# A hybrid encoder layer: seven-product parts for blocks 0 to 11 of the first down-projection, and all weight sums on GpSimd

## The chip, the cores and the metric

The kernel runs on one core of a Trainium2 chip. TensorE multiplies matrices and accumulates them in the banks of PSUM; VectorE, ScalarE and GpSimd work on tiles in SBUF; SyncE (SP) issues most of the DMA transfers, ScalarE some. The metric is the device time of one execution in microseconds (us), as the median of several runs.

## What is computed

One layer of a streaming encoder, in float32, over 2112 tokens (a prompt of 2048 and a sample of 64), with 1024 features and a hidden width of 2816:

```python
mod = (c_act @ w_ada + b_ada)[:, None, :]
sh1, sc1, gt1, sh2, sc2, gt2 = jnp.split(mod, 6, -1)
h = rmsnorm(x, g1) * (1 + sc1) + sh1
proj = h @ w_in                                  # pooling inputs u, and q, k, v, o, gates
pool_out, pool_buf_new = pool_mixer(u, pool_buf, start, w_pool, s_pool)
hs, C, n, m = mlstm_seq(q, k * HEAD_DIM ** -0.5, v, ig, lf, C, n, m)
...
mix = jnp.concatenate([pool_out, hs], -1) @ w_out
x = x + gt1 * mix                                # end of the attention half
h2 = rmsnorm(x, g2) * (1 + sc2) + sh2
up = h2 @ w_up                                   # (T, 2 * 2816)
conv = b_conv + sum(w_conv[j] * upp[:, j:j + T] for j in range(3))
a, g = jnp.split(conv, 2, -1)
x = x + gt2 * ((jax.nn.silu(g) * a) @ w_down)    # the down-projection
```

The states of the pooling mixer, the mLSTM and the convolution are outputs too.

## The kernel before, in words

Features lie on the partitions and tokens along the rows. Every weight is split into two rounded parts, high and low, so that a float32 product is three passes of the fast format: ScalarE copies the high part (L428), VectorE subtracts to get the low part (L431).

**The attention half** takes the tokens in four groups, three of 512 and a last of 576. Within a group come the projections, the four mLSTM heads, the pooling mixer, and the output projection, which runs two rows of 128 features at a time (eight rows; 16 units of weights `wo_in` and `w_out`, loaded by SP into `raw`). For each row x is loaded (`scr<-xT`, L608), the product is added to it on VectorE, the row is stored (`x2d<-scr`, L661), and its squares are summed into `ssum` (L522 for row 0, L525 and L526 for the others). A pair of rows takes the four PSUM banks `mm`, two for each row, so row 5 uses the banks that row 3's addition sets free. In this half a scheduler orders the instructions of each engine from the program's order and its own estimates; what is marked `keep_in_program_order` keeps its place.

Side work is written as generators in five lists, `bg[0]` to `bg[4]`. A tick takes one step of a list's first generator, and `drain` runs lists until they are empty. `bg[4]` holds `up_sums` from the second group on. It makes the sums of weights that the Strassen products of the FFN's up-projection need: 22 blocks of two column halves are 44 pieces, each with two loads of `w_up` into a tile `w4` (four buffers), four sums of 128x256, and a store to `wsum` in HBM. Three pieces are loaded ahead.

**From attention to FFN.** After the matmuls of rows 0 and 1 of the last group's output projection, `between()` is called, which there is `leave()`: it drains the lists 1 to 4, gives the attention half's memory back (the pool `a1`, with `w4` in it, among it), opens the FFN's pool `f1` in that memory, and appends `norm_sums`. That one makes the sums of the first FFN group's operands: for each of four column pairs it loads `h2d` into `fscr` (issued by ScalarE, L829), and makes seven operands, each with two high copies on ScalarE (L809 into `hx`) and low parts and differences on VectorE (L795, L791).

**The FFN half** takes the tokens in three groups of 704, which are three squares of two halves of 352. In this half the order of all engines is written out by hand. The up-projection of each of the 22 blocks takes seven products instead of eight (L1616). The down-projection is done in parts of blocks, listed in `PARTS`. A part of four blocks is done in seven products too (`Quad`, `quad_down`, L2084): 168 matmuls of 352 columns, with weight sums `dsum`. A part of six is an ordinary product (L2230): 288 matmuls, alternately of 448 and 256 columns. The first group has the parts (0, 6), (6, 12), (12, 16), (16, 22); the other two have (0, 4), (4, 8), (8, 12), (12, 16), (16, 22). The weight sums `dsum` are made in the first group by `quad_sums`: 16 pieces, each with one load from `w_quad` into a tile `qs`, four sums of 128x256 on VectorE, and a store to `dsum` (the lists `SUMS` say which are made when).

Of the kernel before, what the change touches and what calls it, by code (L numbers as in the profile page):

```python
# [9 lines left out]
F32 = mybir.dt.float32  # L10
F32R = mybir.dt.float32r
# [5 lines left out]
P = 128  # L17
# [7 lines left out]
NF = 22  # L25
# [7 lines left out]
PARTS = (((0, 6), (6, 12), (12, 16), (16, 22)), ((0, 4), (4, 8), (8, 12), (12, 16), (16, 22)),  # L33
         ((0, 4), (4, 8), (8, 12), (12, 16), (16, 22)))
NQ, QUADS = 4, 4
SUMS = ((6, 7, 0, 1, 2), (3, 4, 5))
# [30 lines left out]
def tile_layer(ctx: ExitStack, tc: tile.TileContext, xT, vecs, cst, rst, w_mod, w_ada, w_qkou, w_v, w_pool,  # L67
# [799 lines left out]
    if True:  # L867
# [6 lines left out]
        def up_sums():  # L874

            def load(f, c):
                w = a1.tile([P, 4, 256], F32, tag="w4", name="w4", bufs=4)
                for i in range(2):
                    tc.keep_in_program_order(nc.sync.dma_start(out=w[:, 2 * i:2 * i + 2, :], in_=w_up[NF * i + f].rearrange(
                        "p (h c) -> p h c", h=2)[:, :, c:c + 256]))  # L880
                return w
            todo = [(f, c) for f in range(NF) for c in (0, 256)]
# [3 lines left out]
            def store():  # L886
                if made:
                    f, c, w = made.pop()
                    pin(nc.sync.dma_start(out=wsum[f, :, :, c:c + 256], in_=w))
            yield  # L890
            yield
            for i, (f, c) in enumerate(todo):
                w = nx.pop(0)
                yield
                yield

                a0, a1_, g0, g1 = (w[:, i, :] for i in range(4))
                pin(dve.tensor_tensor(out=g1, in0=g0, in1=g1, op=ALU.add))
                pin(dve.tensor_tensor(out=g0, in0=a0, in1=g0, op=ALU.subtract))
                yield  # L900
                store()
                pin(dve.tensor_tensor(out=a0, in0=g1, in1=a0, op=ALU.subtract))
                pin(dve.tensor_tensor(out=a1_, in0=a1_, in1=a0, op=ALU.subtract))
                made.append((f, c, w))
                yield
                if 0 < i and i + 2 < len(todo):
                    nx.append(load(*todo[i + 2]))
# [758 lines left out]
    def quad_sums(ds):  # L1666

        for d in ds:
            for c in (0, 256):
                t = f2.tile([P, 2, FT], F32R, tag="av", name="qs", bufs=AVB)  # L1670
                w = t.bitcast(F32).rearrange("p a t -> p (a t)")[:, :1024].rearrange("p (i c) -> p i c", i=4)
                nc.sync.dma_start(out=w, in_=w_quad[d, :, :, c:c + 256])
                for _ in range(7):
                    yield
                a11, a12, a21, a22 = (w[:, i] for i in range(4))
                dve.tensor_tensor(out=a22, in0=a21, in1=a22, op=ALU.add)
                yield
                dve.tensor_tensor(out=a21, in0=a11, in1=a21, op=ALU.subtract)
                yield
                dve.tensor_tensor(out=a11, in0=a22, in1=a11, op=ALU.subtract)  # L1680
                yield
                dve.tensor_tensor(out=a12, in0=a12, in1=a11, op=ALU.subtract)
                yield
                yield
                nc.sync.dma_start(out=dsum[d, :, :, c:c + 256], in_=w)
                yield
                yield

# [474 lines left out]
    for o in fgroups:  # L2163
        Bo = B[o.g]
        held = None
        for pi, part in enumerate(PARTS[o.g]):
# [6 lines left out]
            if quad is not None and o.g == 0:  # L2173
                drain(0)
                aside, bg[1][:] = list(bg[1]), []
            if pi == 0:
                pair = None
            for f in range(f0, f1_):
                old, pair = pair, Pair(o, Bo, f, f - f0, av, quad)
                pair.products(old)  # L2180
                if o.g == 0 and f == 2:
                    bg[0].append(quad_sums(SUMS[0]))
# [3 lines left out]
                if held is not None and nf > 2:  # L2186
                    quad_down(o, held, pair, old)
                    held = None
                    if o.g == 0:
                        bg[0].append(quad_sums(SUMS[1]))  # L2190
                        bg[1].extend(aside)
# [199 lines left out]
```

## Time and profile before

| | |
|---|---|
| time, median of 3 runs | 2168.68 us (2167.97 to 2169.99) |
| span of the profiled execution | 2165.8 us; the page gives no other time of its own for it, and the median of the runs is 2.9 us above |
| TensorE busy | 2143.9 us, 99% |
| VectorE, ScalarE busy | 1649.8 and 1105.2 us, 76% and 51% |
| GpSimd busy | 265.3 us, 12% |
| the attention half ends | with the output projection's last matmul, at 787.0 us |

A row of a profile gives a line of the kernel, an engine, an operation, the tiles out and in, and a count; then the busy time and the mean of one in ns, and the idle time ahead of them with what ended it. In a timeline the first number is the start in us and the second the length. "<-" in brackets names what an engine had waited for. The lines shown with an L are those of the kernel before.

### The profile page before, as it was taken

Reading aid. Unit: us, or ns where it says so; the run is one execution under the profiler, and the core shown is the slowest. Engines: PE = TensorE matmul, PEld = TensorE weight load, DVE = VectorE, ACT = ScalarE, POOL = GpSimd, SP = SyncE. Lnnn points to the kernel's source line nnn. Section 1 sums busy time; section 2 is a strip of 40 time slices with the busy share of each in tenths; the row PEclk is TensorE's granted clock in tenths of the full one; section 3 lists DMA queues with packets and bytes.
Section 4 is the critical chain, followed back from the end, with each engine's and each line's share of the span. In section 5 each row is a group of like instructions: output and inputs, shape, how many; then the busy total and the mean of one; then the engine's idle time right before and its main releaser. Section 6 shows DMA issues by size and latency. Waiting matters only on the chain.

```text
span 2165.8 us, 38050 instructions
## 1 busy us (share of the span) xinstructions
PE 2143.9 (99%) x13529; PEld 2038.3 (94%) x13529; DVE 1649.8 (76%) x3060; ACT 1105.2 (51%) x2193; POOL 265.3 (12%) x475
## 2 busy tenths in 40 slices
PE   8999999999999999999999999999999999999998
PEld 7888888888899999999999999999999999999998
DVE  5777679677675778788688768988877597887874
ACT  4554335234333557465556445655655365565554
POOL 0010000001000301010001220100101321111112
PEclk9999999999999999999999999999999999999999
DMA  8987997897799689797768976665668675555542
GB/s 320 331 304 225 325 311 249 292 325 259 247 294 296 207 273 317 241 343 248 229 219 305 360 282 207 228 225 202 219 234 276 221 251 190 171 175 188 172 159 76
DMA packets 297063, 541.09 MB, mean 250 GB/s; under 512 B 25728, under 2 KB 113280, under 8 KB 296872
## 3 DMA queue, kind: packets, MB, share of 16 engines
q1 hardware_dynamic: 286280, 513.44, 70.3%
q10 hardware_dynamic: 10592, 25.20, 3.0%
q8 instruction: 107, 1.75, 0.3%
q14 instruction: 84, 0.69, 0.1%
HBM read 412.56 MB, written 125.98 MB: 249 GB/s over the span
## 4 chain that ended last, share of the span: by engine, by line
PE 89%; DVE 4%; DMA 3%; issue 1%; ACT 1%; SPq 0%; POOL 0%; POOLq 0%; DVEq 0%; ACTq 0%
PE mm L1616 37%; PE mm L495 23%; PE mm L2230 11%; PE mm L2084 10%; PE mm L1155 3%; DVE wt L431 1%; PE m L1345 1%; PE m L1365 1%; PE m L1367 1%; PE m L1330 1%; DMA wt<-dsum 0%; PE mm L1091 0%; DMA qs<-w_quad 0%; DVE tg L1594 0%; DMA raw<-w_up 0%
## 5 line engine op out<-in xcount | busy, mean ns | idle before, releaser
L1616 PE MATMUL mm<-hx,wt 128*128 128x352 f32 x5544 | 886.1, 321 | 2.5 <-DVE wt L431 2.2
L1616 PEld LDWEIGHTS mm<-hx,wt 128*128 128x128 f32 x5544 | 878.3, 188 | 4.9 <-DVE wt L431 4.2
L495 PE MATMUL mm<-hl,wt 128*128 128x512 f32 (+2 forms) x1920 | 385.4, 356 | 0.0
L431 DVE TENSOR_TENSOR wt<-raw,wt 128x512 fp32r<-128x512 f32 (+1 forms) x460 | 310.8, 681 | 79.1 <-ACT wt L428 77.7
L428 ACT ACTIVATE wt<-raw 128x512 fp32r<-128x512 f32 (+1 forms) x460 | 274.7, 604 | 168.0 <-PE mm L495 53.2
L495 PEld LDWEIGHTS mm<-hl,wt 128*128 128x128 f32 x1920 | 314.7, 188 | 47.4 <-issue 4.4
L2084 PE MATMUL mm<-av,wt 128*128 128x352 f32 x1512 | 248.0, 323 | 1.7 <-DVE x L2053 0.7
L2084 PEld LDWEIGHTS mm<-av,wt 128*128 128x128 f32 x1512 | 242.3, 188 | 4.8 <-DVE ea L1625 2.8
L2230 PE MATMUL mm<-av,wt 128*128 128x448 f32 (+1 forms) x1440 | 231.4, 322 | 0.0
L2053 DVE SCALAR_TENSOR_TENSOR x<-mm,MOD,x 128x352 f32<-128x352 f32 (+3 forms) x368 | 171.9, 507 | 77.8 <-PE mm L2230 62.0
L2230 PEld LDWEIGHTS mm<-av,wt 128*128 128x128 f32 x1440 | 220.8, 188 | 9.7
L1664 ACT ACTIVATE mm<-mm 128x352 f32<-128x352 f32 x204 | 91.4, 448 | 238.9 <-PE mm L1616 175.1
L495 PE MATMUL mm<-mx,wt 128*128 128x512 f32 (+1 forms) x960 | 182.6, 352 | 0.0
L495 PEld LDWEIGHTS mm<-mx,wt 128*128 128x128 f32 x960 | 159.3, 188 | 22.5
L1594 DVE SCALAR_TENSOR_TENSOR ta<-ea,V,ta 128x704 f32<-128x704 f32 (+1 forms) x132 | 125.7, 953 | 60.4 <-ACT ta L1589 56.3
L1594 DVE SCALAR_TENSOR_TENSOR tg<-eg,V,tg 128x704 f32<-128x704 f32 (+1 forms) x132 | 125.7, 952 | 49.8 <-ACT tg L1589 47.2
L431 DVE TENSOR_TENSOR wt<-wt 128x512 fp32r<-128x512 f32 x204 | 138.7, 685 | 10.9 <-ACT wt L428 10.7
L428 ACT ACTIVATE wt<-wt 128x512 fp32r<-128x512 f32 x204 | 123.8, 622 | 25.9 <-DMA wt<-wsum 24.7
L1572 POOL COPY ea<-UC 128x2 f32<-128x2 f32 x66 | 35.0, 530 | 529.1 <-DVE ta L1594 418.4
L1812 ACT ACTIVATE tg<-tg 128x704 f32<-128x704 f32 (+1 forms) x66 | 52.5, 796 | 71.3 <-DVE tg L1594 71.3
L1155 PE MATMUL mm<-wt,hl 128*128 128x256 f32 (+1 forms) x576 | 71.2, 284 | 0.0
L1155 PEld LDWEIGHTS mm<-wt,hl 128*128 128x128 f32 x576 | 70.3, 189 | 0.8 <-issue 0.6
(305 smaller groups left out, 2222.7 us busy)
## 6 DMA issues: line engine op xcount, KB each, us to landing
wt<-wsplit SPq DMA_DIRECT2D x132, 512.0 KB, 4.2
raw<-w_up SPq DMA_DIRECT2D x198, 256.0 KB, 4.1
wt<-hl_kept SPq DMA_DIRECT2D x96, 512.0 KB, 5.9
wt<-wsum SPq DMA_DIRECT2D x132, 256.0 KB, 4.9
wsplit<-wt SPq DMA_DIRECT2D x66, 512.0 KB, 5.3
w<-w_up SPq DMA_DIRECT2D x88, 256.0 KB, 4.7
wsum<-w SPq DMA_DIRECT2D x44, 512.0 KB, 5.3
Bd<-fscr ACTq DMA_DIRECT2D x56, 352.0 KB, 3.4
```

The costliest lines, as they stand in the source:

```text
L428: act.activation(u.w[:, 0, :u.n], u.raw[:, :u.n], AF.Copy)
L431: dve.tensor_tensor(out=u.w[:, 1, :u.n], in0=u.raw[:, :u.n], in1=u.w[:, 0, :u.n].bitcast(F32), op=ALU.subtract)
L495: pe.matmul(ps[bi][:, :hi - lo], U[:, a, k % 4 * P:(k % 4 + 1) * P], mv[k][:, b, lo:hi], start=(at == 0 and pi == 0), stop=(k == order[-1] ...
L1155: pe.matmul(ps[ti][:n, :cols], h[4 * kh + k4][:, b, lo:lo + n], U[:, a, k4 % 2 * cols:(k4 % 2 + 1) * cols], start=(kh == 0 and k4 == 0 and ...
L1572: pool.tensor_copy(ext[:, 0:2], UC[:, f, :])
L1594: dve.scalar_tensor_tensor(out=t[:, :E], in0=ext[:, j:j + E], scalar=wc(j, f), in1=t[:, :E], op0=ALU.mult, op1=ALU.add)
L1616: pe.matmul(bk.t[:, :FH], U[:, a, kc * P:(kc + 1) * P], Bo.at(nm, kc, b), start=(first and kc == 0 and pi == 0), stop=(kc == 3 and pi == 2 ...
L1664: act.activation(to.t[:, :FH], bk.t[:, :FH], AF.Copy)
L1812: act.activation(self.tg[:, :E], self.tg[:, :E], AF.Silu)
L2053: dve.scalar_tensor_tensor(out=x3[n][:, a:b], in0=bk.t[:, a - lo:b - lo], scalar=gt2(n, s), in1=x3[n][:, a:b], op0=ALU.mult, op1=ALU.add)
L2084: pe.matmul(bk.t[:, :FH], U[:, a, c:c + P], quad.put(op, m, b), start=(first and m == 0 and pi == 0), stop=(m == 1 and pi == 2), skip_grou ...
L2230: pe.matmul(bks[i].t[:, :hi - lo], U[:, a, k % 4 * P:(k % 4 + 1) * P], av[k][:, b, lo:hi], start=(k == 0 and (a, b) == PASSES[0]), stop=(k ...
```

## The change

The first FFN group gets the same parts as the other two, so blocks 0 to 11 become three seven-product parts in place of two ordinary ones. `quad_sums` and its lists go; the 16 pieces of `w_quad` are appended to `up_sums`, behind its 44, with the same tile, one load each and a store to `dsum`. All its sums, of both kinds, are given to GpSimd in place of VectorE. The operands of the second FFN group (`prepare`) are no longer put aside while the first group's `dsum` are finished.

```diff
--- before.py
+++ after.py
@@ -30,10 +30,9 @@
 EB = 1
 AVB = 7
 ENDS = ((0, 448), (448, 704))
-PARTS = (((0, 6), (6, 12), (12, 16), (16, 22)), ((0, 4), (4, 8), (8, 12), (12, 16), (16, 22)),
+PARTS = (((0, 4), (4, 8), (8, 12), (12, 16), (16, 22)), ((0, 4), (4, 8), (8, 12), (12, 16), (16, 22)),
          ((0, 4), (4, 8), (8, 12), (12, 16), (16, 22)))
 NQ, QUADS = 4, 4
-SUMS = ((6, 7, 0, 1, 2), (3, 4, 5))
 
 
 def paired(g, part):
@@ -875,18 +874,22 @@
 
             def load(f, c):
                 w = a1.tile([P, 4, 256], F32, tag="w4", name="w4", bufs=4)
+                if f >= NF:
+                    tc.keep_in_program_order(nc.sync.dma_start(out=w, in_=w_quad[f - NF, :, :, c:c + 256]))
+                    return w
                 for i in range(2):
                     tc.keep_in_program_order(nc.sync.dma_start(out=w[:, 2 * i:2 * i + 2, :], in_=w_up[NF * i + f].rearrange(
                         "p (h c) -> p h c", h=2)[:, :, c:c + 256]))
                 return w
-            todo = [(f, c) for f in range(NF) for c in (0, 256)]
+            todo = [(f, c) for f in range(NF + 2 * QUADS) for c in (0, 256)]
             pin = tc.keep_in_program_order
             nx, made = [load(*todo[i]) for i in range(3)], []
 
             def store():
                 if made:
                     f, c, w = made.pop()
-                    pin(nc.sync.dma_start(out=wsum[f, :, :, c:c + 256], in_=w))
+                    to = wsum[f] if f < NF else dsum[f - NF]
+                    pin(nc.sync.dma_start(out=to[:, :, c:c + 256], in_=w))
             yield
             yield
             for i, (f, c) in enumerate(todo):
@@ -895,12 +898,12 @@
                 yield
 
                 a0, a1_, g0, g1 = (w[:, i, :] for i in range(4))
-                pin(dve.tensor_tensor(out=g1, in0=g0, in1=g1, op=ALU.add))
-                pin(dve.tensor_tensor(out=g0, in0=a0, in1=g0, op=ALU.subtract))
+                pin(pool.tensor_tensor(out=g1, in0=g0, in1=g1, op=ALU.add))
+                pin(pool.tensor_tensor(out=g0, in0=a0, in1=g0, op=ALU.subtract))
                 yield
                 store()
-                pin(dve.tensor_tensor(out=a0, in0=g1, in1=a0, op=ALU.subtract))
-                pin(dve.tensor_tensor(out=a1_, in0=a1_, in1=a0, op=ALU.subtract))
+                pin(pool.tensor_tensor(out=a0, in0=g1, in1=a0, op=ALU.subtract))
+                pin(pool.tensor_tensor(out=a1_, in0=a1_, in1=a0, op=ALU.subtract))
                 made.append((f, c, w))
                 yield
                 if 0 < i and i + 2 < len(todo):
@@ -1662,29 +1665,6 @@
     def seed(to, bk):
 
         act.activation(to.t[:, :FH], bk.t[:, :FH], AF.Copy)
-
-    def quad_sums(ds):
-
-        for d in ds:
-            for c in (0, 256):
-                t = f2.tile([P, 2, FT], F32R, tag="av", name="qs", bufs=AVB)
-                w = t.bitcast(F32).rearrange("p a t -> p (a t)")[:, :1024].rearrange("p (i c) -> p i c", i=4)
-                nc.sync.dma_start(out=w, in_=w_quad[d, :, :, c:c + 256])
-                for _ in range(7):
-                    yield
-                a11, a12, a21, a22 = (w[:, i] for i in range(4))
-                dve.tensor_tensor(out=a22, in0=a21, in1=a22, op=ALU.add)
-                yield
-                dve.tensor_tensor(out=a21, in0=a11, in1=a21, op=ALU.subtract)
-                yield
-                dve.tensor_tensor(out=a11, in0=a22, in1=a11, op=ALU.subtract)
-                yield
-                dve.tensor_tensor(out=a12, in0=a12, in1=a11, op=ALU.subtract)
-                yield
-                yield
-                nc.sync.dma_start(out=dsum[d, :, :, c:c + 256], in_=w)
-                yield
-                yield
 
     def half_tile(nm):
         return f1.tile([P, FH], F32, tag=nm, name=nm)
@@ -2170,25 +2150,18 @@
             ends = o.last and lastp
             av = [None] * nf
             quad = Quad() if paired(o.g, part) else None
-            if quad is not None and o.g == 0:
-                drain(0)
-                aside, bg[1][:] = list(bg[1]), []
             if pi == 0:
                 pair = None
             for f in range(f0, f1_):
                 old, pair = pair, Pair(o, Bo, f, f - f0, av, quad)
                 pair.products(old)
                 if o.g == 0 and f == 2:
-                    bg[0].append(quad_sums(SUMS[0]))
                     bg[1].append(prepare(fgroups[1], fscr))
                 if o.g == 0 and len(x3) < KD or pi == 0 and not bg[0]:
                     x3 += load_x2(o, range(len(x3), min(len(x3) + 2, KD)))
                 if held is not None and nf > 2:
                     quad_down(o, held, pair, old)
                     held = None
-                    if o.g == 0:
-                        bg[0].append(quad_sums(SUMS[1]))
-                        bg[1].extend(aside)
             if pi == 0 and o.g > 0:
                 drain(0)
                 x3 += load_x2(o, range(len(x3), KD))
```

What the change does to the order of the instructions shows at the passage from attention to FFN. In the new kernel the lines of the same code have numbers a few lower; `w_7815`, `w_8001` and so on are tiles `w4`, each holding one piece.

GpSimd in the new kernel, where the pooling mixer of the last group ends:

```order
L1429 COPY PO<-u 128x15
L1430 COPY PO<-u 128x15
L901 TENSOR_TENSOR w_7815<-w_7815 128x256
L902 TENSOR_TENSOR w_7815<-w_7815 128x256
L905 TENSOR_TENSOR w_7815<-w_7815 128x256
L906 TENSOR_TENSOR w_7815<-w_7815 128x256
L901 TENSOR_TENSOR w_8001<-w_8001 128x256
L902 TENSOR_TENSOR w_8001<-w_8001 128x256
```

In this manner it goes on for 64 sums, down to the piece `w_8283`; in the kernel before, the FFN's first instruction (a memset of `UC`) stands in this place.

SP at the same passage, before, from the last store into `wsum` on:

```order
L889 DMA wsum<-w_7587 512x1x256
L771 DMA h2d<-mx_6358 128x352
L1458 DMA o_pool<-PO 128x120
L608 DMA scr<-xT 128x576
L407 DMA raw<-w_out 128x512
L407 DMA raw<-wo_in 128x512
L407 DMA raw<-w_out 128x512
L407 DMA raw<-wo_in 128x512
L661 DMA x2d<-scr 128x576
L407 DMA raw<-w_out 128x512
L661 DMA x2d<-scr 128x576
L608 DMA scr<-xT 128x576
```

SP in the new kernel, where the load of x for row 2 is followed by the first store into `dsum`:

```order
L1461 DMA o_pool<-PO 128x120
L607 DMA scr<-xT 128x576
L892 DMA dsum<-w_7815 512x1x256
L878 DMA w_8199<-w_quad 128x4x256
L892 DMA dsum<-w_8001 512x1x256
L878 DMA w_8206<-w_quad 128x4x256
```

and the end of the same run:

```order
L878 DMA w_8276<-w_quad 128x4x256
L892 DMA dsum<-w_8262 512x1x256
L878 DMA w_8283<-w_quad 128x4x256
L892 DMA dsum<-w_8269 512x1x256
L892 DMA dsum<-w_8276 512x1x256
L892 DMA dsum<-w_8283 512x1x256
L660 DMA x2d<-scr 128x576 x2
L607 DMA scr<-xT 128x576
L660 DMA x2d<-scr 128x576
L406 DMA raw<-wo_in 128x512
L406 DMA raw<-w_out 128x512
L406 DMA raw<-wo_in 128x512
```

Sixteen stores and thirteen loads now stand ahead of the stores of rows 0 and 1, the load of x for row 3, and the last five loads of the output projection's weights.

ScalarE, before, where the loads of `norm_sums` come (`mx` and `u` belong to the attention half, `wt` to the weights' split):

```order
L517 ACTIVATE mx_7615<-scr 128x576
L428 ACTIVATE wt<-raw 128x512
L517 ACTIVATE mx_7614<-scr 128x576
L829 DMA fscr<-h2d 128x704 x4
L428 ACTIVATE wt<-raw 128x512
L809 ACTIVATE hx<-fscr 128x352 x4
L428 ACTIVATE wt<-raw 128x512
L522 ACTIVATE ssum<-scr 128x576
```

and in the new kernel:

```order
L427 ACTIVATE wt<-raw 128x512
L516 ACTIVATE mx_7614<-scr 128x576
L427 ACTIVATE wt<-raw 128x512 x4
L524 ACTIVATE scr<-scr 128x576
L521 ACTIVATE ssum<-scr 128x576
L828 DMA fscr<-h2d 128x704 x4
L808 ACTIVATE hx<-fscr 128x352 x2
L427 ACTIVATE wt<-raw 128x512
```

The loads `fscr<-h2d` and all copies of `norm_sums` have moved behind the squares of rows 0 and 1 (L524, L521). The instruction at L521 waits there for the last transfer of every DMA queue ahead of it, the last store into `dsum` among them, and for GpSimd's last sum.

## The prediction

> **What bounds the kernel now.** I read the page's head with its list of engines, then the waits of TensorE, then the windows.
>
> ```profile
> span 2165.8 us, 38050 instructions
> PE 2143.9 (99%) x13529; PEld 2038.3 (94%) x13529; DVE 1649.8 (76%) x3060; ACT 1105.2 (51%) x2193; POOL 265.3 (12%) x475
> ```
> The waits of TensorE (sum, count and mean in us):
> ```profile
> PE m L1054 <- DMA mx<-xT: 5.5, 1, 5.5
> PE mm L1616 <- DVE wt L431: 2.2, 3, 1.1
> ```
> TensorE is idle for 2165.8 − 2143.9 = 22 us of the span, and its longest waits are of this size. So matmuls taken away shorten the time one for one, as long as everything that feeds them stays ahead; and a feed that comes late shows in full. The median of the runs, 2168.7, is 2.9 us over the span of the profiled execution; I work in the span and add the 2.9.
>
> **What is removed from TensorE.** The chain that ended last has, of the opening group, the first ordinary part of six blocks (L2230) and its part of four in seven products (L2084):
>
> ```profile
> 867.03 3.88 PE mm L2230 x24
> ...
> 872.81 41.99 PE mm L2230 x264
> ...
> 1105.31 4.03 PE mm L2084 x24
> ...
> 1111.24 23.05 PE mm L2084 x144
> ```
> Blocks 0 to 11 cost 2 × (3.88 + 41.99) = 91.7 us before, and 3 × (4.03 + 23.05) = 81.2 us after: **−10.5 us**. Nothing else covers TensorE there, so all of it counts.
>
> **The sums on GpSimd.** The 176 sums of w_up leave VectorE (four lines of this kind), the 64 of w_quad leave it in the opening FFN group, and all 240 go to GpSimd. VectorE's price is the first row, from the lines between 220 and 740 us; GpSimd's are its only two-input groups of this size:
>
> ```profile
> L902 DVE TENSOR_TENSOR w<-w 128x256 f32<-128x256 f32 x44 | 18.6, 422 | 0.8
> ```
> ```profile
> L2045 POOL TENSOR_TENSOR ssum<-ssum,fscr 128x256 f32<-128x256 f32 x4 | 2.9, 736 | 8.8 <-ACT fscr L2044 8.8
> ...
> L2033 POOL TENSOR_TENSOR y<-x,fscr 128x256 f32<-128x256 f32 x2 | 1.4, 726 | 2.0 <-ACT fscr L2001 2.0
> ```
> A piece is four sums: 4 × 0.422 = 1.7 us on VectorE, 4 × 0.726 = 2.9 us on GpSimd, which gets 240 × 0.726 = 174 us of work. The windows of core 0 (columns: window, length, then PE, PEld, DVE, ACT and POOL, then clock, DMA share, GB/s):
>
> ```profile
> 220.00:740.00 520.00, 519.24 (x3197) 460.10 (x3196) 379.20 (x822) 204.00 (x515) 45.48 (x56) 1.00 0.85 280
> 1041.00:1105.00 64.00, 64.00 (x406) 63.92 (x405) 48.61 (x74) 41.39 (x76) 8.22 (x16) 1.00 0.72 235
> ```
> For 220 to 740, where the 44 pieces of w_up lie, TensorE already runs 519.24 of 520 us, so the 176 × 0.42 = 74 us that VectorE sheds can win under 1 us. It can lose: two operations side by side are slow in this trace.
>
> ```profile
> 722.96 8.33 POOL L1426 COPY PO<-u 128x15 f32<-128x15 f32 x1 [1.20 <-ACT u L267]
> ...
> 738.93 0.80 POOL L1427 COPY PO<-u 128x15 f32<-128x15 f32 x1
> ```
> ```profile
> 1228.13 1.71 POOL L2045 TENSOR_TENSOR ssum<-ssum,fscr 128x704 f32<-128x704 f32 x1 [2.39 <-ACT fscr L2044]
> ```
> ```profile
> 1228.54 1.84 DVE L431 TENSOR_TENSOR wt<-raw,wt 128x512 fp32r<-128x512 f32 x1 [1.05 <-ACT wt L428]
> ```
> The same split takes 0.69 us as a rule (x14, from the lines between 740 and 800 us):
>
> ```profile
> L431 DVE TENSOR_TENSOR wt<-raw,wt 128x512 fp32r<-128x512 f32 x14 | 9.6, 686 | 6.3 <-ACT wt L428 6.3
> ```
> Beside GpSimd's add it took 1.84, 1.16 more. If one in ten of the 176 sums cost TensorE that much, it is 20 us. Bounds −1 to +20; VectorE has 27% of this stretch idle, so I take **+2**. The Trainium skill has the same rule (GPSIMD Engine Reference, section Key points): GpSimd shares its SBUF interfaces with VectorE and contends with VectorE instructions of two SBUF inputs. The trace agrees, and the rule speaks against this change; what it would make of it is rival C.
>
> In the opening FFN group VectorE loses 64 × 0.42 = 27 us of sums, and takes on the handling of three seven-product parts for two ordinary ones. The window from 1041 to 1105 shows such a group's work at 48.6 of 64 us with TensorE never idle. I take 0, with +5 as the upper end; work of the next group's operands now lies over these parts.
>
> **Sixteen pieces of w_quad do not fit into the attention half.** This is the large term. The order of the new kernel shows that 13 of the 16 come out as one run where the last attention group hands over to the FFN half: on GpSimd behind the last copy into PO, 64 sums in a row; on SP a store of dsum and a load of w_quad in turns, each store waiting for GpSimd, each load for an older store (four buffers). SP issues in order, and behind this run stand the row x2d and scr<-xT of row 3, and five of the output projection's 16 weight loads. On ScalarE, L521 (square sum) waits for all DMA under way and for GpSimd's last sum, because the FFN's pool takes the memory of the w4 tiles; behind it stand the loads fscr<-h2d and the copies of norm_sums, which makes the FFN's first operands. What stands there before:
>
> ```profile
> 739.76 0.34 SPq L1458 DMA_DIRECT2D o_pool<-PO  x1
> ...
> 753.52 0.42 SPq L608 DMA_DIRECT2D scr<-xT  x1
> ...
> 754.04 0.42 SPq L407 DMA_DIRECT2D raw<-wo_in  x1
> ```
> ```profile
> 735.76 51.36 PE L495 MATMUL mm<-mx,wt 128*128 128x256 f32 x384
> 786.96 2.08 PE L1616 MATMUL mm<-hx,wt 128*128 128x352 f32 x12
> 789.03 10.61 PE L1616 MATMUL mm<-hx,wt 128*128 128x352 f32 x66
> ```
> ```profile
> 742.19 2.22 ACTq L829 DMA_DIRECT2D fscr<-h2d  x4
> 747.39 0.50 ACT L809 ACTIVATE hx<-fscr 128x352 fp32r<-128x352 f32 x1 [2.24 <-DMA fscr<-h2d]
> ...
> 786.11 0.87 ACT L809 ACTIVATE hx<-fscr 128x352 fp32r<-128x352 f32 x2
> ```
> SP is free of the projection's loads at 754; norm_sums runs from its load at 742.2 to about 787, 45 us, and ends just as TensorE wants it (786.96).
>
> *When the run ends.* Its first sum comes behind 738.93 + 0.80 = 739.7. Lower bound: 16 × 2.9 = 46.5 us of GpSimd alone, to 786.2, and 3.4 for the last store to land, 789.6. Upper: with four buffers a piece goes round in a store (5.3), a load (6.1) and the sums (2.9), 14.3 us per four, 3.6 each; three pieces to about 751.7, 13 more to 798.2, and 5.3 to land, 803.5. The landings, from the page and from the tile qs:
>
> ```profile
> wsum<-w SPq DMA_DIRECT2D x44, 512.0 KB, 5.3
> ```
> ```profile
> DMA to landing us min/median/max: 3.4/6.1/8.5
> ```
> I take 3.2 us per piece, about 793, and with the landing an end E ≈ 797.
>
> The Trainium skill (GPSIMD Engine Reference, section Instruction dispatch) has some 2.5 cycles for an element of two inputs; at its 1.2 GHz a sum would be 533 ns, an estimate, the pieces 34 us and the time about 2190; the rows' 726 ns include what each instruction costs beside its elements, and I go by them.
>
> *What TensorE does meanwhile.* Its 16 units of the projection take 51.36 / 8 = 6.42 us for a row of x. It can run rows 0 to 4, to 735.8 + 5 × 6.42 = 767.9; row 5 needs the banks of row 3, whose addition needs the x that SP loads behind the run. So it stops from about 768 to E + 2.5 (behind E come a weight's copy on ScalarE, 0.62, its split, 0.69, and a row's addition, 1.15, below).
>
> *How late the FFN starts.* Rows 5 to 7 are 19.3 us, so with norm_sums quick the FFN starts at E + 21.8 against 786.96: a delay of E − 765. With norm_sums as long as before, counted from E, the first block's six products end at E + 47 against 789.03 + 10.61 = 799: a delay of E − 752. What VectorE and ScalarE do there, from the lines between 740 and 800 us:
>
> ```profile
> L795 DVE TENSOR_TENSOR hx<-fscr,hx 128x352 fp32r<-128x352 f32 x28 | 13.5, 521 | 0.3 <-ACT hx L809 0.3
> ...
> L791 DVE TENSOR_TENSOR fscr<-fscr 128x352 f32<-128x352 f32 x16 | 8.1, 520 | 0.0
> L267 DVE SCALAR_TENSOR_TENSOR scr<-mm,MOD,scr 128x256 f32<-128x256 f32 x16 | 7.0, 479 | 1.1 <-PE mm L495 1.1
> L526 DVE TENSOR_TENSOR ssum<-ssum,scr 128x576 f32<-128x576 f32 x7 | 5.3, 756 | 1.0 <-ACT scr L525 1.0
> ...
> L267 DVE SCALAR_TENSOR_TENSOR scr<-mm,MOD,scr 128x64 f32<-128x64 f32 x8 | 2.2, 277 | 0.0
> ```
> ```profile
> L428 ACT ACTIVATE wt<-raw 128x512 fp32r<-128x512 f32 x12 | 7.5, 621 | 2.9 <-DMA raw<-w_out 1.8 <-DVE hx L795 1.1
> ```
> norm_sums is 13.5 + 8.1 = 21.6 us of VectorE; a row of x is (7.0 + 2.2) / 8 = 1.15 for the addition and 0.76 for the square sum. Behind E wait norm_sums, five rows (9.6) and 11 splits for the projection's rest and the FFN's first weights (7.5): 39 us, nearer the long end than the short one. I take E − 755 = **+42 us**. Bounds: 789.6 − 765 = 24.6 and 803.5 − 752 = 51.5.
>
> Sum: 2165.8 − 10.5 + 2 + 0 + 42 = 2199.3, and with 2.9 outside the span **2202 us**.
>
> **Rivals.**
> A, the forecast: the run of 13 pieces holds up SP and ScalarE, and norm_sums starts only behind it: 2168.7 − 10.5 + 2 + 24.6 = 2185 to 2212 (with 51.5) by the bounds.
> B, only SP's part counts, because norm_sums catches up while TensorE does rows 5 to 7: +27 instead of +42, about 2187. For it: VectorE has little else to do from 768 on. Against: 39 us of its work do not fit into 22.
> C, the shared port is what costs, on top of A: 176 sums beside VectorE's splits make the attention half 15 to 30 us longer, 2217 to 2232. For it: the 8.33 us copy and the 1.84 us split. Against: in 45 us of GpSimd's work there TensorE lost under 1 us.
> D, the other side: the run ends early enough to be hidden, and the gain stands, 2168.7 − 10.5 = 2158. That needs its last store landed by about 765, thus 16 pieces in some 20 us, 1.3 us each, under half of GpSimd's price; or L521 and the loads not held up. It decides when E is below 775, where delay and gain cancel. Against: 16 × 2.9 alone reaches 786.
> E, VectorE becomes the bound in the three new parts and eats the 10.5: 2213. Against: its 76% in the window.
>
> **How the numbers follow.** A 0.60, B 0.15, C 0.12, D 0.06, E 0.07. The likeliest gives 2202. The range 2182 to 2224 takes in A and B whole, E, and the lower half of C, and leaves out D and the worst of C, under 2 in 10. A measurement of this kernel tells some 0.2%, 4.3 us. Faster is D, 0.05; within 0.2% is the small stretch of E near 775, 0.02; slower is the rest, 0.93.
>
> **What the profile after would show.** SP's queue with dsum and w_quad in turns from about 740 to 795, nothing between. TensorE idle for some 30 us from about 768, released by SP's load of x or by the row additions, and idle again or slow in the FFN's first block until E + 45. ScalarE's L521 waiting on a DMA into dsum for about 45 us. GpSimd's busy time up by 174 us or more (more shows C, in sums longer than 0.73 us). L2084 with 504 matmuls more and L2230 with 576 fewer. The step on the end of the run is wrong if TensorE stops for less than 10 us between 735 and 830; the step on the port is wrong if TensorE loses more than 5 us before 735; that on TensorE's gain, if a seven-product part takes more than 28 us in the opening group.

## The result: 3.1% slower, and the profile after

The changed kernel takes 2236.1 us (median of 4 runs) against 2169.3 for the kernel before; the ratio is 1.031, with a 95% interval of 1.030 to 1.033. The direction was forecast, the size was not: 2202, with a range that ended at 2224.

The head of the page of the kernel after, and TensorE's longest waits in it (sum, count and longest in us):

```profile
span 2234.4 us, 38147 instructions
PE 2151.2 (96%) x13457; PEld 2042.4 (91%) x13457; DVE 1654.7 (74%) x2912; ACT 1128.9 (51%) x2245; POOL 481.5 (22%) x715
```
```profile
PE mm L494 <- DVE scr L266: 37.9, 3, 35.6
PE m L1348 <- DVE kw L266: 8.3, 2, 4.3
...
PE mm L2064 <- DVE ea L1628: 4.5, 4, 1.5
```

TensorE has 72 matmuls fewer and is idle for 83 us in place of 22. The three waits belong to three places, which the rest of this text keeps apart: the passage to the FFN (L494), the heads of the attention half (L1348), and the seven-product parts of the opening group (L2064).

To compare kernels, the span is cut at three matmuls of TensorE: the start of the last output projection, the row sum that follows the FFN's first six products, and the row sum that follows the part (16, 22) of the opening group. The timelines of TensorE, after and then before:

```profile
750.87 32.16 PE L494 MATMUL mm<-mx,wt 128*128 128x256 f32 x240
818.60 5.24 PE L494 MATMUL mm<-mx,wt 128*128 128x256 f32 x28 [35.57 <-DVE scr L266]
...
867.15 1.15 PE L534 MATMUL m<-ones_r,ssum 128*128 128x1 f32 x10
...
1323.91 1.38 PE L1915 MATMUL m<-ones_r,ssum 128*128 128x1 f32 x12
```
```profile
799.48 1.15 PE L535 MATMUL m<-ones_r,ssum 128*128 128x1 f32 x10
...
1254.10 1.38 PE L1935 MATMUL m<-ones_r,ssum 128*128 128x1 f32 x12
```

Cut in this way, the 68.6 us by which the span grew come from (all in us):

| kernel | attention half | passage | opening group | rest | span |
|---|---|---|---|---|---|
| before | 735.8 | 63.7 | 454.6 | 911.7 | 2165.8 |
| after | +15.1 | +52.6 | +2.1 | −1.2 | 2234.4 |

The opening group's +2.1 holds the 10.5 us that the matmuls should have saved: 12.6 us went the other way. The windows of that group, before and after (columns as in the prediction: length, then TensorE busy and its count):

```profile
799.50:1254.10 454.60, 452.90 (x2847) 445.27 (x2847) 360.99 (x592) 260.62 (x468) 60.13 (x96) 1.00 0.83 283
```
```profile
867.20:1323.90 456.70, 447.06 (x2775) 439.42 (x2774) 384.63 (x620) 285.19 (x519) 62.53 (x96) 1.00 0.76 257
```

TensorE is idle for 9.6 us of it in place of 1.7, and busy for 5.8 us less instead of 10.5: its matmuls took longer in the mean.

**The run of pieces** is in the trace as forecast. GpSimd, from the last copy into PO on, and the end of it:

```profile
755.38 0.80 POOL L1430 COPY PO<-u 128x15 f32<-128x15 f32 x1
756.15 1.18 POOL L901 TENSOR_TENSOR w<-w 128x256 f32<-128x256 f32 x1
...
785.59 0.72 POOL L902 TENSOR_TENSOR w<-w 128x256 f32<-128x256 f32 x1
786.39 0.72 POOL L905 TENSOR_TENSOR w<-w 128x256 f32<-128x256 f32 x1
...
815.23 0.17 POOL L1558 MEMSET UC<- 128x88 f32 x1 [3.35 <-DMA dsum<-w]
```

SP, at the run's end:

```profile
804.79 7.63 SPq L892 DMA_DIRECT2D dsum<-w  x3
...
814.12 0.73 SPq L607 DMA_DIRECT2D scr<-xT  x1
```

The memset of UC is the first write into the memory taken over, so its start marks the end of the run, E = 815.2 us. A sum takes 0.72 us, starts 0.8 after the one before, and with the waits for loads a piece comes to (815.2 − 3.4 − 756.2) / 16 = 3.5 us. TensorE stops at 783.0 and resumes at 818.6, 3.4 us behind E. What stands ahead of that on ScalarE and on VectorE:

```profile
815.27 0.69 ACT L521 ACTIVATE ssum<-scr 128x576 f32<-128x576 f32 x1 [49.15 <-DMA dsum<-w]
```
```profile
815.99 0.76 DVE L525 TENSOR_TENSOR ssum<-ssum,scr 128x576 f32<-128x576 f32 x1 [44.80 <-ACT ssum L521]
817.97 1.07 DVE L266 SCALAR_TENSOR_TENSOR scr<-mm,MOD,scr 128x256 f32<-128x256 f32 x3 [1.22 <-DMA scr<-xT]
```

The row's addition (L266), for which TensorE waits, was held twice: it stands in VectorE's order behind a square sum that waits for ScalarE's L521, until 816.8, and then it waits another 1.2 us for the x that SP loads. The second wait was forecast, the first was not.

**The heads.** VectorE in the new kernel, ahead of TensorE's first stop, and TensorE there:

```profile
277.65 1.21 DVE L224 SCALAR_TENSOR_TENSOR s<-raw,CA,s 128x512 f32<-128x512 f32 x1
...
279.92 1.21 DVE L947 TENSOR_TENSOR ssum<-ssum,mx 128x512 f32<-128x512 f32 x1
281.05 0.74 DVE L224 SCALAR_TENSOR_TENSOR s<-raw,CA,s 128x512 f32<-128x512 f32 x1
281.71 0.74 DVE L224 SCALAR_TENSOR_TENSOR acc<-raw,CA,acc 128x512 f32<-128x512 f32 x1
282.37 0.68 DVE L266 TENSOR_TENSOR kw<-m,CL 128x512 f32<-128x512 f32 x1
```
```profile
283.10 2.09 PE L1348 MATMUL m<-va,kw 128*128 128x129 f32 x8 [4.03 <-DVE kw L266]
```

Operations of 128x512 take 1.21 us while GpSimd's sums run (till 280.6) and 0.74 or less once they have ended. kw, for which TensorE waits, is the last line. The lines ahead of it are side work (sums for the modulation and for the norm), not the head's; from 267.4 us on twelve such operations of 1.21 to 1.23 us stand in a row in VectorE's queue, and so kw comes some 4 us late. The windows of core 0 (columns as in the prediction; the clock is the third number from the end) show what follows such a stop:

```profile
279.00:283.00 4.00, 0.08 (x1) 0.00 (x0) 4.00 (x6) 0.11 (x1) 1.50 (x2) 0.90 1.03 364
283.00:286.00 3.00, 2.90 (x11) 2.70 (x12) 2.81 (x7) 0.64 (x1) 0.00 (x0) 0.50 1.07 395
286.00:289.00 3.00, 3.00 (x9) 2.32 (x8) 2.37 (x5) 0.00 (x0) 0.00 (x0) 0.50 1.08 396
289.00:292.00 3.00, 3.00 (x23) 2.79 (x22) 0.54 (x2) 1.08 (x6) 0.00 (x0) 0.99 0.94 342
```

For 6 us behind the stop TensorE runs at half clock, which costs another 3. Stop and slow stretch together put TensorE 6.5 us further behind the kernel before; at the second stop, of 4.29 us, it is 5.4. The two are 11.9 of the 15.1 us. The Trainium skill (TensorE: Matmul & The Clock Gate, section Part 1: The HAM clock gate) has half rate after an idle window of some 3.4 us, and the full rate again after as long a busy one; the trace agrees on the stop (4.03 us), and behind it the half rate lasted some 6 us.

### The profile page after: what moved, and what is told of

Read it like the earlier page. It is cut to its first block, busy times and chain, and to the rows that moved or that the text cites. A ratio compares the mean times of both kernels' runs of the same rounds, so it can differ in the third digit from the quotient of the medians.

```text
span 2234.4 us, 38147 instructions
## 1 busy us (share of the span) xinstructions
PE 2151.2 (96%) x13457; PEld 2042.4 (91%) x13457; DVE 1654.7 (74%) x2912; ACT 1128.9 (51%) x2245; POOL 481.5 (22%) x715
## 4 chain that ended last, share of the span: by engine, by line
PE 75%; DVE 9%; DMA 7%; issue 4%; POOL 2%; ACT 2%; SPq 0%; DVEq 0%; POOLq 0%; ACTq 0%
PE mm L1619 32%; PE mm L494 16%; PE mm L2064 12%; PE mm L2203 6%; PE mm L1158 3%; DVE wt L430 2%; DMA wt<-wsum 1%; DMA scr<-xT 1%; DMA wt<-dsum 1%; DVE tg L1597 1%; PE m L1348 1%; DMA dsum<-w 1%; POOL w L901 1%; DMA wsplit<-wt 1%; PE m L1368 1%
## 5 line engine op out<-in xcount | busy, mean ns | idle before, releaser
L494 PE MATMUL mm<-hl,wt 128*128 128x512 f32 (+2 forms) x1920 | 388.4, 358 | 0.2 <-ACT va L266 0.2
L430 DVE TENSOR_TENSOR wt<-raw,wt 128x512 fp32r<-128x512 f32 (+2 forms) x446 | 311.1, 703 | 74.1 <-ACT wt L427 73.9
L494 PEld LDWEIGHTS mm<-hl,wt 128*128 128x128 f32 x1920 | 316.9, 189 | 48.5 <-issue 4.4
L2064 PE MATMUL mm<-av,wt 128*128 128x352 f32 x2016 | 332.0, 324 | 7.7 <-DVE ea L1628 4.5
L2064 PEld LDWEIGHTS mm<-av,wt 128*128 128x128 f32 x2016 | 323.0, 188 | 13.4 <-DVE ea L1628 8.4
L427 ACT ACTIVATE wt<-raw 128x512 fp32r<-128x512 f32 (+2 forms) x446 | 269.4, 611 | 125.7 <-PE mm L494 32.7
L2033 DVE SCALAR_TENSOR_TENSOR x<-mm,MOD,x 128x352 f32<-128x352 f32 (+5 forms) x408 | 193.9, 518 | 56.0 <-PE mm L2203 39.1
L494 PE MATMUL mm<-mx,wt 128*128 128x512 f32 (+2 forms) x960 | 188.5, 359 | 42.8 <-DVE scr L266 37.9
L494 PEld LDWEIGHTS mm<-mx,wt 128*128 128x128 f32 x960 | 163.5, 194 | 67.1 <-issue 36.2
L430 DVE TENSOR_TENSOR wt<-wt 128x512 fp32r<-128x512 f32 x228 | 155.0, 687 | 2.7 <-ACT wt L427 2.7
L427 ACT ACTIVATE wt<-wt 128x512 fp32r<-128x512 f32 x228 | 139.6, 623 | 22.4 <-DMA wt<-wsum 16.4
L2203 PE MATMUL mm<-av,wt 128*128 128x448 f32 (+1 forms) x864 | 139.0, 322 | 0.0
L1575 POOL COPY eg<-UC 128x2 f32<-128x2 f32 x66 | 30.9, 468 | 223.2 <-DVE tg L1597 214.1
L901 POOL TENSOR_TENSOR w<-w 128x256 f32<-128x256 f32 x60 | 54.6, 910 | 97.9 <-DMA w<-w_up 95.1
```

The source lines that it names most:

```text
L427: act.activation(u.w[:, 0, :u.n], u.raw[:, :u.n], AF.Copy)
L430: dve.tensor_tensor(out=u.w[:, 1, :u.n], in0=u.raw[:, :u.n], in1=u.w[:, 0, :u.n].bitcast(F32), op=ALU.subtract)
L494: pe.matmul(ps[bi][:, :hi - lo], U[:, a, k % 4 * P:(k % 4 + 1) * P], mv[k][:, b, lo:hi], start=(at == 0 and pi == 0), stop=(k == order[-1] ...
L901: pin(pool.tensor_tensor(out=g1, in0=g0, in1=g1, op=ALU.add))
L1575: pool.tensor_copy(ext[:, 0:2], UC[:, f, :])
L2033: dve.scalar_tensor_tensor(out=x3[n][:, a:b], in0=bk.t[:, a - lo:b - lo], scalar=gt2(n, s), in1=x3[n][:, a:b], op0=ALU.mult, op1=ALU.add)
```

## The experiments

All of them in the same cut, as differences to the kernel before (us, from each one's profile):

| run | attention half | passage | opening group | rest | time (median) |
|---|---|---|---|---|---|
| the kernel after | +15.1 | +52.6 | +2.1 | −1.2 | 2236.1 |
| e1, sums of w_up on GpSimd alone | +16.7 | +2.3 | +1.8 | +1.1 | 2185.6 |
| e10, copies in their place | −0.4 | +1.6 | +1.1 | −0.2 | 2169.4 |
| e2, after with all sums on VectorE | −1.0 | +47.9 | +2.6 | −0.7 | 2217.9 |
| e3, after with one piece left at the passage | +17.9 | +7.6 | +2.5 | −2.2 | 2195.5 |
| e9, after with 9 pieces at the passage | +28.9 | +31.3 | +1.3 | −0.4 | 2227.7 |
| e4, as e3, sums on VectorE | +7.4 | +11.4 | +3.0 | −1.6 | 2186.3 |
| e5, pieces' transfers off SP | +14.5 | +116.3 | +2.3 | −0.5 | 2300.9 |
| e6, on VectorE, from the first group on | +34.6 | +5.4 | +1.9 | −1.1 | 2209.0 |
| e7, as e6, prepare from block 6 | +39.3 | +4.9 | +5.3 | −0.6 | 2211.6 |
| e8, as e6, prepare from block 10 | +34.2 | +5.1 | +32.7 | −1.3 | 2238.7 |

### The attention half: GpSimd's second input

The theory was that GpSimd's sums slow VectorE at the heads; the rival, that the pieces of w_quad and the order they bring do it. The first run gives the sums of w_up alone to GpSimd.

```diff
 # the kernel before
-                pin(dve.tensor_tensor(out=g1, in0=g0, in1=g1, op=ALU.add))
+                pin(pool.tensor_tensor(out=g1, in0=g0, in1=g1, op=ALU.add))
...   the other three sums alike
```

> The kernel before, with the 176 sums of w_up on GpSimd and nothing else changed. Theory (GpSimd's sums and VectorE's two-input operations slow each other, VectorE comes late for a head's kw and TensorE stops some 4 us twice, with half clock behind it): TensorE starts the last output projection 12 to 16 us later than before (735.8 us), VectorE's 128x512 operations in the heads take up to 1.2 us beside sums of over 1 us, and the time is 2181 to 2186. Rival (the 16 pieces of w_quad, or the order that they bring, delay the attention half): no stop of TensorE at the heads, time 2167 to 2171.

Measured: ratio 1.0078 (1.0064 to 1.0091), the last projection 16.7 us late, and the same two stops:

```profile
PE m L1345 <- DVE kw L267: 8.3, 2, 4.3
```

So neither w_quad nor the new parts are needed for this loss. What VectorE gains by it is small: in the kernel before it is busy for 379 us between 220 and 740 us, 74 of them sums. Here, over the same work, it is

```profile
220.00:755.00 535.00, 523.32 (x3180) 462.74 (x3179) 355.67 (x643) 197.87 (x509) 207.97 (x229) 0.99 0.81 270
```

356 us: of the 74 us that were taken from it, about 50 came back as longer operations. GpSimd's side of it, over the same stretch:

```profile
L899 POOL TENSOR_TENSOR w<-w 128x256 f32<-128x256 f32 x44 | 46.8, 1063 | 3.4
L898 POOL TENSOR_TENSOR w<-w 128x256 f32<-128x256 f32 x44 | 41.8, 949 | 96.0 <-DMA w<-w_up 96.0
```

Is it the second input, or only something more in GpSimd's queue? The next run puts copies of one operand in the place of the sums; the sums are left out, so that wsum holds other numbers.

```diff
 # e1
-                pin(pool.tensor_tensor(out=g1, in0=g0, in1=g1, op=ALU.add))
+                pin(pool.tensor_copy(g1, g0))
...   the other three sums alike
```

> The kernel before with the 176 sums of w_up replaced by 176 copies of one operand, 128x256, on GpSimd, at the same places with the same loads and stores; the sums themselves are left out. Theory (the second input is what makes GpSimd and VectorE slow each other): VectorE's 128x512 operations stay at their 0.74 us, TensorE's two stops at the heads' kw go, the attention half loses 0 to 4 us, time 2167 to 2174. Rival (it is GpSimd's queue or the order that delays VectorE): the two stops stay, and the time is 2179 or more.

Measured: ratio 1.0005 (0.9996 to 1.0015); the wait for kw is gone, and the attention half is as long as before. GpSimd and VectorE between 220 and 755 us:

```profile
L899 POOL COPY w<-w 128x256 f32<-128x256 f32 x44 | 33.2, 755 | 2.7
L898 POOL COPY w<-w 128x256 f32<-128x256 f32 x44 | 25.7, 584 | 96.5 <-DMA w<-w_up 96.5
```
```profile
L225 DVE SCALAR_TENSOR_TENSOR s<-raw,CA,s 128x512 f32<-128x512 f32 x42 | 32.7, 779 | 0.0
```

The copies wait for the same loads and take 63% of the sums' time (105.6 us against 166.7, all four lines of each); VectorE's operation of the modulation sums (L225), of the kind that stands ahead of kw, has a mean of 779 ns here, 868 in e1 and 743 before. A copy is shorter as well as simpler, so the second input and the mere length of the overlap aren't told apart to the end; place and queue are ruled out.

### The passage: how long the run of pieces is, and what it holds up

```diff
 # the kernel after
-                pin(pool.tensor_tensor(out=g1, in0=g0, in1=g1, op=ALU.add))
+                pin(dve.tensor_tensor(out=g1, in0=g0, in1=g1, op=ALU.add))
...   the other three sums alike
```

> The changed kernel with all 240 sums on VectorE; 13 of the 16 pieces of w_quad still come out at the passage. Theory of the port: the last output projection starts at 735 to 738 as before. Theory of the run of pieces: it stays, but its length is set by the transfers (a load, 1.7 us of sums, a store, four buffers), some 2.5 to 3.2 us per piece in place of 3.3; the passage still costs 20 to 35 us, the opening group stays 1 us longer than before, time 2190 to 2205. If the attention half's loss came from the order and the loads instead, it stays at 15 us and the time is above 2205.

Measured: ratio 1.0232 (1.0217 to 1.0248), 2217.9 us. The attention half is back at −1.0 us, as the theory of the port had it. The passage is not: 47.9 us, against 20 to 35 expected, and with it the time lies above its range. GpSimd's first write behind the run, and TensorE:

```profile
795.79 0.17 POOL L1558 MEMSET UC<- 128x88 f32 x1 [57.30 <-DMA dsum<-w]
```
```profile
798.51 8.99 PE L494 MATMUL mm<-mx,wt 128*128 128x256 f32 x48 [29.19 <-DVE scr L266]
```

E comes at 795.8, 61.0 us behind the last projection's start; in the kernel after it is 64.4. A piece's sums are 1.2 us shorter on VectorE, but the run is then set by the transfers, which follow each other in the chain that ended last:

```profile
747.38 6.01 DMA w<-w_quad
...
756.27 3.92 DMA dsum<-w
...
760.21 5.14 DMA w<-w_quad
...
765.35 4.74 DMA dsum<-w
```

And norm_sums waits as before, since its work on VectorE stands behind the same E.

The next run is to make all 60 pieces in the attention half, by one step fewer for each.

```diff
 # the kernel after
                 w = nx.pop(0)
                 yield
-                yield
```

> The changed kernel with one step fewer for each piece, so that all 60 pieces are made in the attention half and none at the passage; the sums stay on GpSimd. Theory (the passage's 53 us are the run of pieces): the FFN starts as soon after the last projection as before (51 us), the attention half loses 15 to 22 us by the port, the opening group is 1 us longer, time 2184 to 2192. Rival (the passage is late for another reason, such as the memory taken over from the attention half): the passage still costs over 30 us, time above 2210.

Measured: ratio 1.0124 (1.0110 to 1.0137), 2195.5 us. The passage costs 7.6 us in place of 52.6: the run of pieces was 45 of it. The time is 3.5 us above the range, since the passage was expected as before. The attention half pays 17.9 for 60 pieces at GpSimd, where 44 cost 15.1. One piece is still behind the last copy into PO:

```profile
763.31 1.33 POOL L905 TENSOR_TENSOR w<-w 128x256 f32<-128x256 f32 x1
768.47 0.17 POOL L1557 MEMSET UC<- 128x88 f32 x1 [3.82 <-DMA dsum<-w]
```

SP loads an x behind its store, and TensorE stops for 4.05 us up to 771.4. That is a part of the 7.6; the rest was not looked into.

The step between, where every second piece has one step fewer:

```diff
 # the kernel after
                 w = nx.pop(0)
                 yield
-                yield
+                if i % 2:
+                    yield
```

> The changed kernel with one step fewer for every second piece, so that 9 pieces have their sums at the passage in place of 16. Theory (the passage ends some 50 us behind the last store into dsum, and each piece moves that by GpSimd's 3.25 us): 7 x 3.25 = 23 us less, the passage costs 26 to 34 us more than before (52.6 with 16, 7.6 with none), time 2206 to 2216. Rival (the delay is a fixed price of the memory taken over late, whatever stands ahead): over 42 us, time above 2222.

Measured: ratio 1.0274 (1.0256 to 1.0292), 2227.7 us. The passage is +31.3, inside the 26 to 34 expected; 1, 9 and 16 pieces behind the last copy into PO give 7.6, 31.3 and 52.6, which is 3.0 us for a piece on both steps. The time as a whole missed its range, because the attention half lost 28.9 us in place of 15: with the pieces' new pace came four waits for loads that SP issues (`hl_kept`, the activations kept in HBM):

```profile
PE mm L494 <- DMA wt<-hl_kept: 14.0, 4, 5.6
```

Which of the two things that the run holds up is to blame, SP's loads or ScalarE's L521? Here GpSimd issues the pieces' transfers itself.

```diff
 # the kernel after: load and store of a piece of w_quad
-                    tc.keep_in_program_order(nc.sync.dma_start(out=w, in_=w_quad[f - NF, :, :, c:c + 256]))
+                    tc.keep_in_program_order(nc.gpsimd.dma_start(out=w, in_=w_quad[f - NF, :, :, c:c + 256]))
...
-                    pin(nc.sync.dma_start(out=to[:, :, c:c + 256], in_=w))
+                    pin((nc.sync if f < NF else nc.gpsimd).dma_start(out=to[:, :, c:c + 256], in_=w))
```

> The changed kernel with the loads and stores of the 16 pieces of w_quad issued by GpSimd's own queue, so that SP has nothing of them: its loads of x and of the projection's weights go out as before. ScalarE's L521 and the loads of norm_sums behind it still wait for the last store. Theory (either of the two holds TensorE by itself: ScalarE's wait is enough): TensorE still stops some 30 us in the last output projection, the passage is 45 to 60 us longer than before, time 2228 to 2245. Rival (SP's blocked loads are what holds TensorE): the stop in the projection is gone, and the passage costs 25 us or less, time below 2212.

Measured: ratio 1.0612 (1.0595 to 1.0629), 2300.9 us, outside both ranges. TensorE:

```profile
763.66 0.38 PE L494 MATMUL mm<-mx,wt 128*128 128x256 f32 x1 [0.34 <-DVE scr L266]
764.33 32.12 PE L494 MATMUL mm<-mx,wt 128*128 128x320 f32 x239 [0.29 <-DVE scr L266]
892.46 1.47 PE L1619 MATMUL mm<-hx,wt 128*128 128x352 f32 x3 [96.02 <-ACT hx L808]
```

and GpSimd's memset behind the run:

```profile
888.55 0.17 POOL L1558 MEMSET UC<- 128x88 f32 x1 [2.90 <-DMA dsum<-w]
```

With SP free, 336 of the 384 matmuls run without the long stop: on that point the rival was right. It doesn't show SP's hold by itself, though: in e5 the scheduler also put the additions of the next rows ahead of the square sum L525 on VectorE, and six copies of weights ahead of L521 on ScalarE (767.7 to 783.7 us), which in the kernel after stand behind them. TensorE then stands for 96 us at the FFN's first product, which needs norm_sums; ScalarE's wait is enough to hold the FFN. The run itself became longer, since GpSimd spent about 0.8 us, and for most of them a gap of 1.3 to 3.9, on each transfer (8 to 11 us for a piece), and E came at 888.5. The end of the first six products is 51.9 us behind E in the kernel after, 50.6 in e2, 53.3 in e9, and 41.8 here, where most of the projection was done by then. So ScalarE's path is real without SP's, the passage is E plus what norm_sums takes, and how much SP alone would have cost stays open. To free ScalarE alone, the tiles of the pieces would need memory that the FFN doesn't take over, and there was not enough; this was not tried.

### The opening group: VectorE with `prepare` beside it

```diff
 # e3
-                pin(pool.tensor_tensor(out=g1, in0=g0, in1=g1, op=ALU.add))
+                pin(dve.tensor_tensor(out=g1, in0=g0, in1=g1, op=ALU.add))
...   the other three sums alike
```

> The same as the one with one step fewer for each piece, and all sums on VectorE. Theory: no loss at the port, none at the passage; what is left is the opening group, where the 10.5 us of fewer matmuls are eaten by stops of TensorE for VectorE. Time 2167 to 2172, the opening group's four seven-product parts with 2 to 3 us of stops each. If VectorE cannot take 64 sums more in the attention half, 2175 or more; if the opening group's stops came from the late passage, the gain shows and the time is 2158 to 2162.

Measured: ratio 1.0076 (1.0064 to 1.0089), 2186.3 us. With neither the port nor a run of pieces, the opening group is still 3.0 us longer than before, so its stops don't come from the late passage. The attention half does lose here (7.4 us), and the passage 11.4. VectorE's 389 of 520 us, against 379 before, with the sums bunched, may be why, but no trace shows it: TensorE's longest stop there, 5.2 us in the FFN's first block, is for ScalarE. So I spread the sums, beginning in the first attention group, and in two more runs began `prepare` (the second group's operands, 32 us of VectorE) later.

```diff
 # e2                                            (e6)
-            if o.g == 1:
+            if o.g == 0:
                 bg[4].append(up_sums())
 # e6                                            (e7; e8 with f == 10)
-                if o.g == 0 and f == 2:
+                if o.g == 0 and f == 6:
                     bg[1].append(prepare(fgroups[1], fscr))
```

> All sums on VectorE, at their old pace, but begun in the first attention group in place of the second; all 60 pieces end well ahead of the passage. Theory: VectorE's 27 us more are spread over 735 us, the attention half loses 0 to 4 us, the passage 0 to 4, the opening group's four seven-product parts keep their stops (2 to 3 us longer than before in spite of 10.5 us fewer matmuls), time 2168 to 2177. If the loss of the version with one step fewer came from the pieces' number and not from their pace, 2180 or more.

> The last one, with the second group's operands (prepare) begun at block 6 in place of block 2. Theory (in the opening group VectorE is full with prepare beside the seven-product parts): the first of these parts has no stop, the last part has more to do, which its 28 of 48 us leave room for; 2 to 4 us less than the last one. If VectorE is full without prepare, no difference.

> The same with prepare begun at block 10. Theory: the first two seven-product parts have no stops, 4 to 7 us less than with block 2, as long as prepare still ends before the last part's products do; what is left then is made in one go, and costs 2 to 8 us there.

Measured: 2209.0, 2211.6 and 2238.7 us (ratios 1.0182, 1.0195, 1.0325; intervals of 0.003 to 0.004). All three missed their times, in the first attention group. TensorE's waits there, of e6:

```profile
PE mm L494 <- ACT wt L427: 10.1, 5, 3.7
PE mm L1402 <- DVE nd L266: 5.8, 3, 3.5
```

The loss there, 34 to 39 us in the three, was not followed further. The opening group of the FFN is what these runs are for. The time from one seven-product part's end to the next one's (the first counted from the row sum):

| run | (0, 4) | (4, 8) | (8, 12) | (12, 16) |
|---|---|---|---|---|
| after, prepare from block 2 | 85.9 | 84.1 | 84.5 | 85.0 |
| e6, from block 2 | 86.3 | 84.1 | 83.9 | 85.0 |
| e7, from block 6 | 82.6 | 84.2 | 84.1 | 84.4 |
| e8, from block 10 | 82.6 | 81.1 | 84.2 | 85.6 |

Where prepare is not beside it, a part takes 3.0 to 3.7 us less, and only there. The windows fit that; (4, 8) in the kernel after, and in e8 (length, then TensorE, its weight loads, VectorE, ScalarE):

```profile
931.00:1014.00 83.00, 80.64 (x500) 79.49 (x501) 75.56 (x126) 55.18 (x102) 9.58 (x16) 1.00 0.73 248
```
```profile
902.00:985.00 83.00, 83.00 (x518) 82.68 (x517) 71.65 (x117) 51.59 (x95) 8.89 (x16) 1.00 0.64 214
```

VectorE is at 91% with prepare and at 86% without, and TensorE loses 2.4 us in the one and none in the other. At 91% small waits for VectorE come at every part. Beginning prepare late doesn't save time in the end: at the end of e8's last part all that is left of prepare is made in one go, and TensorE stands:

```profile
1275.78 3.60 PE L1619 MATMUL mm<-hx,wt 128*128 128x352 f32 x12 [34.62 <-DVE eg L1628]
```

VectorE is busy for only 11 us of this stop; the rest it waits for prepare's loads and for ScalarE's copies. No version that beats the kernel before came out of these runs.

## Why the prediction was wrong in size

Of the 68.6 us, 33.5 were forecast. The rest is three terms, each taken too low:

- **The gain on TensorE, −10.5: right, and eaten.** In e8 a part without prepare takes 81.1 us and TensorE has no stop in it. The step that failed is that on VectorE in the opening FFN group: "I take 0, with +5 as the upper end". It measured 12.6. The step read VectorE's 76% from the window 1041 to 1105, which lies between two parts and holds no prepare; the sentence that followed it, on the next group's operands, named the load and gave it no price. That was rival E, in size (10.5) and cause, except that the old part (12, 16) paid too: it had no stop before, when prepare was put aside there.
- **The attention half, +2: 15.1.** The bounds (−1 to +20) held, the choice in them failed: "VectorE has 27% of this stretch idle". An average over 520 us says nothing of the 15 us ahead of a head's kw. The argument against C, 45 us of GpSimd's work without a loss, failed too: that work held no run of two-input sums. The cause was as C has it, with a second part that the sum had no term for: half clock behind each stop. GpSimd's busy time rose by 216 us, not 174, the sign that the prediction had named for C. The Trainium skill (GPSIMD Engine Reference, section Key points) has GpSimd contend with VectorE instructions of two SBUF inputs; the trace agrees, with 0.74 us grown to 1.21.
- **The end of the run: right, within 3 us.** It was to begin at 739.7 and end 57.3 us later; it began at 756.2, late by the attention half's loss, and ended 59.0 later. TensorE's stop, from the end of row 4 to E + 2.5, is there as forecast (to E + 3.4). That SP and ScalarE are both held up is right as well: L521 waited 49 us. But the stop in the projection was put down to SP's load of x alone, and the trace has the same addition held by ScalarE as well, to within 1.2 us of it; that the time came out right there is in part luck.
- **The FFN's start, +42: 52.6.** Counted from the projection's start, E came 3.2 us later than forecast (64.4 in place of 61.2). The other 7.4 us are the step from E to the FFN: I took E − 755, between E − 765 and E − 752. It came out beyond the long end: the first six products ended at E + 52, not E + 47. TensorE's waits for row additions, splits and norm_sums lie in these 5 us, and the half clock behind the stop of 35.6 us (the 28 matmuls at 818.6 take 187 ns each, against 134 before). The bound, 51.5, had no term for either.
- **The range.** C and E were counted as other ways for it to go. They were not: they lie at other places than A, each with a cause of its own, and all three came true at once. A, C and E together, at the prices that the prediction itself gives (2202, 15 to 30 more, 10.5 more), are 2228 to 2243; the measured 2236 lies in the middle.

Two smaller readings were off, and neither moved the forecast: the third number of TensorE's waits is the longest, not the mean; and rival B's own rule, E − 765, gives +32 with E at 797, about 2192, not +27.

The missing 13.1, 10.6 and 12.6, less 1.2 in the rest, are the 35.1 us between 33.5 and 68.6.

## What to carry to other kernels

Two-input sums given to GpSimd came off VectorE only in part here: 74 us of sums moved gave back 24. Rivals at different places of a kernel add up; a range has to hold their sum. And before side work is appended to a generator, count its steps: what isn't done when the lists are drained becomes one serial run, on every queue that it uses, at the very place where the next stage waits for the memory.

## What had not been expected of the hardware

- One-input copies of 128x256 on GpSimd, 176 of them at the sums' places, cost the kernel nothing that could be measured (1.0005, 0.9996 to 1.0015), though VectorE's operation beside them went from 743 to 779 ns; two-input sums cost 16.5 us (2185.6 against 2169.1).
- A two-input sum on GpSimd takes 0.72 us beside a VectorE that is almost idle and 1.05 to 1.19 beside a busy one; VectorE's operation of 128x512 goes from 0.74 to 1.21 at the same time.
- A stop of TensorE of 4.0 us costs 6.5, since its clock stands at 0.50 for the 6 us that follow.
- A transfer that GpSimd issues holds its queue for about 0.8 us, and between its own sums a gap of 1.3 to 3.9 us lay ahead of most of them, for which the profile mostly names no cause (e5).
